# An RWKV-7 and convolution layer on one core: head pairs given in two parts, the LayerNorm 60 priorities later, the bonus product behind the keys

## The chip, the core and the metric

The kernel runs on one core of one Trainium2 chip. A time is the device time of one execution in microseconds (us). The kernel before took 2864.6 us, the median of three runs (2861.78 to 2865.63). The two kernels compute the same outputs from the same inputs.

## What is computed

One layer works on 2048 new tokens of 1024 channels, and on one token more for each of 8 older sequences. In the reference, cut to what matters here:

```python
h = rms_norm(x, norm_pre_g)
proj = h @ w_in                      # r, k, v, z, two lora inputs, conv input, gates
ps = ps + (ps_prev - ps) * mu_shift  # token shift on r, k, v, z and the lora inputs
w_raw = decay_w0 + tanh(wl) @ decay_w2;  decay = exp(-exp(-softplus(-w_raw) - 0.5))
iclr = sigmoid(iclr_a0 + al @ iclr_a2)
kk = k * k_k;  kk = kk * rsqrt(sum(kk * kk) + 1e-12)       # per head of 64 channels
k = k * (1 + (iclr - 1) * k_a)
# per head, token by token:
# S_t = S_(t-1) diag(w_t) + (S_(t-1) a_t) b_t^T + v_t k_t^T;  y_t = S_t r_t   (a = -kk, b = kk * iclr)
y_gn = group_norm(y_w)
bonus = sum(r * k * r_k) * v                               # per head
o_r = (y_gn + bonus) * silu(z)
c = causal_conv(u * sigmoid(u2), 31 taps);  c = swish(layer_norm(c)) * silu(z_c)
y = sigmoid(g_r) * (o_r @ w_branch_r) + sigmoid(g_c) * (c @ w_branch_c)
x = x + rms_norm(y @ w_out, norm_post_g)
```

## The kernel before

The 2048 tokens are taken in four blocks of 512, and the 16 heads in eight pairs of 128 channels, so there are 32 units of one head pair in one block. Below, "pair 17" is unit 17 of 32, counted from 0: block 2, pair 1. The large products (gemms) run in three passes on a high and a low part of each operand; the weights are split by ScalarE and VectorE in block 0 and read back split in the later blocks. A gemm matmul into a pg bank (`pg<-ht,w`) needs nothing that a pair computes, and so can fill TensorE's time between a pair's steps; "filler" means such matmuls.

`stage_first` normalises block 0: it squares eight tiles of x on ScalarE and sums them over the channels with matmuls by `avg_c` into the bank `py`. `unit_in` computes r, k, v and z of a pair (a gemm and the token shift for each). `unit` does the pair: two small gemms with `lora_w`; the decay as a scan on VectorE (L522); the sum for kk by a matmul with `ones_b` (pa<-tmp,ones_b, the kk statistic); the scaled keys `ar` and `bk`; the bonus statistic (pa<-raw,ones_b) and its product `bonv` with v; silu(z) on ScalarE into a `keep` tile; four transposes of V (pb<-ident,raw); the keys' products (pa<-ar,bk), which VectorE masks into `sc` (sc<-pa,maskw); products into `aw`; transposes of `bk` (pa<-ident,bk), which ScalarE copies into `sc` (sc<-pa); a triangular inverse, done by VectorE row by row (gd, zr, gp; the last transposes are L609 and L611) and by two small products (pb<-gd,sc and pb<-zbuf,gp, the first and second inverse product, with ScalarE's copies gp and zbuf). Its second part is pa<-aw,zbuf, whose results ScalarE copies to pz and xv; pa<-sc,pz; pc<-xv,sc; then the chain of eight chunk states (pc<-xs,aw on TensorE and L691 on VectorE in turn), the outputs into py, and the GroupNorm (py<-gt,cent and pc<-gt,ones_b).

Between the pairs stand the fillers of the lists FILL0 to FILL2: conv inputs ("u"), gates (digits), conv gates ("z", "Z") and the channel LayerNorm of the convolution ("n", `conv_norm`): a matmul with avg_c for the mean (pg<-tmp,avg_c), four subtractions on VectorE, four squares on ScalarE, three adds on VectorE, and a second matmul with avg_c. The 31 taps of the convolution (et<-u,cw,et) are VectorE instructions that `pull` hands out between other steps.

The order on each engine is made by a scheduler at build time, from priorities: what the program gives first goes first when it is ready, `later(n)` moves what it holds n places back, and `behind` lets an instruction be issued only after a given one. Tiles with a tag have a fixed number of buffers (tmp 4, raw 8, keep 4, ar 2, sc 4, xv 2, bk and gd 1); the banks of PSUM are three pg, two pa, one pb, one pc and one py. A new tile of a tag waits until the oldest one is no longer read.

Of the kernel before, what the change touches and what calls it, by code (L numbers as in the profile page):

```python
# [11 lines left out]
ALU = mybir.AluOpType  # L12
# [4 lines left out]
GE, HPO, HPA = 4, 0, 0  # L17
LI = 1000
HP = 550
HPW, HPS, HPG, HPU, HPZ = HP, HP, HP, HP, HP  # L20
# [5 lines left out]
def rwkv7_conformer_step(  # L26
# [362 lines left out]
    def stage_first():  # L389
# [21 lines left out]
        for kt in range(KT):  # L411
            for i, src in enumerate((h9, sh)):
                nc.tensor.transpose(out=psv[:, kt, i, :], in_=src[0:NS, kt * 128:kt * 128 + 128],
                                    identity=ident[0:NS, 0:NS])
        pm = pyt()
        for kt in range(KT):
            sq = new([128, BS], "tmp")
            act(sq, xts[kt], AF.Square)
            mm(pm, avg_c, sq, start=(kt == 0), stop=(kt == KT - 1))
        rb = new([128, BS], "tmp")  # L420
        rsqrt(rb, pm, eps_rms, scale=float(DC) / D)
        ht = [new([128, 2, WX], "ht", F32R) for _ in range(KT)]
# [57 lines left out]
    count = [0]  # L480
    chains = []

# [16 lines left out]

    def unit(b, j, tw, ins):  # L500
        u = count[0]
# [23 lines left out]
        act(em, sw, AF.Exp, scale=DECAY)  # L525
        c3 = lambda t: t.rearrange("p (c t) -> p c t", c=NC)
        act(ep[:, :, 1:C + 1], c3(sw), AF.Exp, scale=-DECAY)
# [16 lines left out]
        stt(R, R, pv("rk", j), K, ALU.mult, ALU.mult)  # L544
        bonv = new([128, BS], "keep")
        mul(bonv, stat(pa, ones_b, R), V)
        sz = new([128, BS], "keep")
# [5 lines left out]
        ps = pb()  # L553
        with behind(*chains[-2:-1]):
            for c2 in range(NC // 2):
                nc.tensor.transpose(out=ps[:, c2 * 128:c2 * 128 + 128], in_=V[:, c2 * 128:c2 * 128 + 128],
                                    identity=ident)
        xv = new([128, NC, 2, C], "xv")
# [84 lines left out]
        for hf in range(2):  # L643
# [6 lines left out]
            for e, es in enumerate(ES):  # L650
                cp(W[hf][es, :, 1, 0:64], psv[ES[1 - e], :, 1, :])

        pull(UT)

# [33 lines left out]
        for c in range(NC):  # L688
            for e, es in enumerate(ES):
                last = mma(pu[es, c * C:c * C + C], MY[es, c, 0, :], xs[es, c, :], False)  # L690
            nc.vector.tensor_scalar(out=state[:, j, :] if c == NC - 1 else xs[:, c + 1, :], in0=pu[:, c * C:c * C + C],  # L691
                                    scalar1=dk[:, c:c + 1], scalar2=None, op0=ALU.mult)
        chains.append(last.ins)
        yps = pyt()
# [431 lines left out]
    def fill(b, ht, cs, what):  # L1126

        if what == "u":
            cs.append(glu(b, ht, len(cs)))
        elif what == "n":  # L1130
            while taps:
                pull(1)
            conv_norm(b, cs)
        elif what in "zZ":
            conv_gate(b, ht, cs, 2 * (what == "Z"))
        else:
            gate(b, ht, 2 * int(what))
# [22 lines left out]
    for b in range(NB):  # L1160
        last = b == NB - 1
        orr = []
        if b == SB - 1:
            work = sample_work()
            act(gate_s, gate_s, AF.Exp, scale=-1.0)
            act(gate_s, gate_s, AF.Ln, bias=1.0)
            act(gate_s, gate_s, AF.Exp, scale=-1.0)
        for j in range(HP):
            if j == RJ and not last:
                stage_rms(b + 1)  # L1170
            orr.append(unit(b, j, tw, ins))
            pull(FT)
            if j < HP - 1:
                ins = unit_in(b, j + 1, ht)
            for what in (FILL0 if b == 0 else FILL2 if last else FILL1)[j]:
                fill(b, ht, cs, what)
                pull(FT)
            if b in DW:
                for _ in range(DW[b][j]):
                    with later(LD):  # L1180
                        next(work, None)
# [81 lines left out]
```

## Time and profile before

| | kernel before |
|---|---|
| median of 3 runs | 2864.6 us (2861.78 to 2865.63) |
| profiled execution, its own time | 2862.01 us |
| its span in the profile | 2860.2 us |
| TensorE matmuls busy (PE) | 2726.3 us, 95% |
| TensorE weight loads busy (PEld) | 2172.7 us, 76% |
| VectorE busy (DVE) | 1967.7 us, 69% |
| ScalarE busy (ACT) | 1319.3 us, 46% |
| mean granted TensorE clock | 0.983 of full speed |

The span is what the profiler shows between the first and the last instruction. The four blocks end at about 745, 1440, 2140 and 2860 us. In a row of the timeline the first number is the start in us from the start of the span, the second the length in us of the merged instructions, then engine, line, operation, the tiles (out<-in) with shapes, the count, and in brackets the idle time of the engine before it and what ended it.

### The profile page before, as it was taken

The numbers are of one execution on the slowest core, as the hardware profiler recorded it, in microseconds if no ns is written. First come the engines' busy times: TensorE is split into PE (matmuls) and PEld (weight loads), VectorE is DVE, ScalarE is ACT, GpSimd is POOL, SyncE is SP. The second block draws the span as 40 slices with busy tenths as digits, with TensorE's granted clock in tenths as the row PEclk, the third lists the DMA queues.
The fourth block names the chain that finished last, engine by engine and source line by source line (L and its number), as shares of the span: only waits on it lengthen the run. The fifth ranks groups of instructions, "written<-read, shape, count | busy, mean of one in ns | idle before, by whom it ended". The sixth has DMA issues, their size and how long they took to land.

```text
span 2860.2 us, 55924 instructions
## 1 busy us (share of the span) xinstructions
PE 2726.3 (95%) x22814; PEld 2172.7 (76%) x22814; DVE 1967.7 (69%) x4553; ACT 1319.3 (46%) x2783; POOL 16.1 (1%) x61
## 2 busy tenths in 40 slices
PE   7999889999999999997999989999999998999998
PEld 6888878877877767775787767777797775777777
DVE  5899896777877567677676677665865856666622
ACT  5555556553244465445213446546512355554521
POOL 0000000000000000000000000000000000000000
PEclk9999999999999999998999999999999998999999
DMA  6555653546874333444565435343465531333474
GB/s 207 198 170 179 207 183 124 185 159 217 304 255 145 101 135 115 136 158 135 168 231 209 136 103 164 107 136 130 161 225 195 202 100 62 107 119 108 154 238 162
DMA packets 157715, 466.91 MB, mean 163 GB/s; under 512 B 19793, under 2 KB 25154, under 8 KB 157451
## 3 DMA queue, kind: packets, MB, share of 16 engines
q1 hardware_dynamic: 154909, 454.23, 47.9%
q10 hardware_dynamic: 2550, 9.12, 0.8%
q8 instruction: 179, 2.93, 0.4%
q14 instruction: 77, 0.63, 0.1%
HBM read 350.41 MB, written 113.35 MB: 162 GB/s over the span
## 4 chain that ended last, share of the span: by engine, by line
PE 60%; DVE 24%; ACT 11%; DMA 3%; issue 2%; SPq 0%; POOL 0%; DVEq 0%; ACTq 0%; POOLq 0%
PE pg L112 36%; PE pa L112 11%; PE pc L112 4%; PE py L112 4%; DVE gd L100 4%; DVE zr L605 4%; DVE zr L106 3%; PE pb L112 2%; ACT tmp L94 2%; ACT sc L94 2%; DVE raw L106 2%; DVE et L106 1%; ACT zbuf L94 1%; ACT gd L94 1%; DVE gp L589 1%
## 5 line engine op out<-in xcount | busy, mean ns | idle before, releaser
L112 PE MATMUL pg<-ht,w 128*128 128x512 f32 (+1 forms) x7200 | 1516.2, 362 | 22.9 <-ACT ht L94 6.6
L112 PEld LDWEIGHTS pg<-ht,w 128*128 128x128 f32 x7200 | 1166.4, 189 | 262.0 <-issue 50.5
L106 DVE SCALAR_TENSOR_TENSOR et<-u,cw,et 128x512 f32<-128x512 f32 x480 | 358.6, 747 | 7.4
L94 ACT ACTIVATE raw<-pg,omm 128x512 f32<-128x512 f32 (+1 forms) x155 | 93.6, 604 | 269.5 <-PE pg L112 263.3
L94 ACT ACTIVATE tmp<-tmp 128x512 f32<-128x512 f32 (+1 forms) x305 | 185.8, 626 | 10.5 <-DVE tmp L522 5.0
L100 DVE TENSOR_TENSOR gd<-zr,gp 128x8 f32<-128x8 f32 (+14 forms) x480 | 179.5, 374 | 12.6
L112 PE MATMUL pg<-orr,w 128*128 128x512 f32 (+2 forms) x960 | 185.9, 350 | 0.0
L605 DVE TENSOR_REDUCE zr<-gd 128x2 f32<-128x8 f32 (+14 forms) x480 | 176.5, 368 | 12.4
L112 PEld LDWEIGHTS pg<-orr,w 128*128 128x128 f32 x960 | 154.8, 188 | 25.8 <-issue 0.5
L94 ACT ACTIVATE w<-wraw 128x512 fp32r<-128x512 f32 x162 | 100.8, 627 | 137.3 <-PE pg L112 92.2
L691 DVE TENSOR_SCALAR xs<-pc,dk 128x64 f32<-128x64 f32 x224 | 63.6, 284 | 122.2 <-PE pc L112 120.0
L100 DVE TENSOR_TENSOR w<-wraw,w 128x512 fp32r<-128x512 f32 x162 | 110.5, 686 | 48.1 <-ACT w L94 43.0
L112 PEld LDWEIGHTS pa<-ar,bk 64*64 64x64 f32 x2048 | 104.3, 137 | 51.0 <-issue 22.8
L106 DVE SCALAR_TENSOR_TENSOR raw<-pg,prm,raw 128x511 f32<-128x511 f32 (+1 forms) x185 | 103.4, 572 | 47.3 <-ACT raw L94 46.7
L112 PE MATMUL pa<-ar,bk 64*64 64x128 f32 x2048 | 128.1, 284 | 6.4 <-DVE keep L100 5.5
L100 DVE TENSOR_TENSOR aw<-pa,id 128x256 f32<-128x256 f32 x64 | 27.2, 424 | 146.3 <-PE pa L112 145.5
L106 DVE SCALAR_TENSOR_TENSOR zr<-zr,sub 128x5 f32<-128x5 f32 (+7 forms) x512 | 115.5, 226 | 13.7
L94 ACT ACTIVATE gd<-sc 32x128 f32<-32x128 f32 x256 | 78.5, 306 | 92.3 <-DVE sc L100 89.5
L94 ACT ACTIVATE x<-pg 128x512 f32<-128x512 f32 (+1 forms) x80 | 40.9, 511 | 169.6 <-PE pg L112 169.3
L100 DVE TENSOR_TENSOR sc<-pa,maskw 128x512 f32<-128x512 f32 x128 | 86.0, 687 | 34.4 <-PE pa L112 33.9
L100 DVE TENSOR_TENSOR x<-x,pg 128x512 f32<-128x512 f32 (+1 forms) x80 | 46.0, 577 | 76.8 <-PE pg L112 65.7
L94 ACT ACTIVATE sc<-pa 64x256 f32<-64x256 f32 (+1 forms) x192 | 72.9, 379 | 42.4 <-PE pb L112 39.4
(357 smaller groups left out, 3740.0 us busy)
## 6 DMA issues: line engine op xcount, KB each, us to landing
w<-kept_in SPq DMA_DIRECT2D x366, 512.0 KB
kept_in<-w SPq DMA_DIRECT2D x122, 512.0 KB
wraw<-in_w_in_dram SPq DMA_DIRECT2D x122, 256.0 KB
w<-kept_br SPq DMA_DIRECT2D x48, 512.0 KB
w<-kept_out SPq DMA_DIRECT2D x40, 512.0 KB
gate<-x SPq DMA_DIRECT2D x64, 256.0 KB
x<-gate SPq DMA_DIRECT2D x64, 256.0 KB
w<-kept_bc SPq DMA_DIRECT2D x24, 512.0 KB
```

Source lines behind the costliest of these rows:

```text
L94: return nc.scalar.activation(out=out, in_=in_, func=func, scale=scale, bias=bias, **kw)
L100: return nc.vector.tensor_tensor(out=out, in0=a, in1=b, op=op)
L106: return nc.vector.scalar_tensor_tensor(out=out, in0=a, scalar=s, in1=b, op0=op0, op1=op1)
L112: return nc.tensor.matmul(out=out, lhsT=lhsT, rhs=rhs, start=start, stop=stop, **kw)
L589: nc.vector.transpose(out=gp, in_=gd.rearrange("p c j -> p j c").unsqueeze(3).to_broadcast([128, 32, NC, 4]))
L605: nc.vector.tensor_reduce(out=zr[:, 0:n, t:t + 2], in_=pr[:, 0:n, :, 0:w], axis=AX.X, op=ALU.add)
L691: nc.vector.tensor_scalar(out=state[:, j, :] if c == NC - 1 else xs[:, c + 1, :], in0=pu[:, c * C:c * C + C], scalar1=dk[:, c:c + 1], scal ...
```

## The change

There are five edits. In `stage_first` the squares are added on VectorE and summed over the channels with one matmul, where eight accumulating matmuls were. `unit` is cut in two functions, `unit_a` up to the transposes of bk and `unit_b` from pa<-aw,zbuf on, and the program gives them in the order: second part of pair j, first part of pair j+1, inputs of pair j+2, fillers of j; before it was both parts of pair j, inputs of j+1, fillers of j. The V transposes no longer stand behind the chain of the pair before the last. The bonus statistic and its product move from ahead of silu(z) to the end of `unit_a`. The LayerNorm of the convolution is put under `later(60)`.

```diff
--- before.py
+++ after.py
@@ -16,6 +16,7 @@
 RJ = 3
 GE, HPO, HPA = 4, 0, 0
 LI = 1000
+LN = 60
 HP = 550
 HPW, HPS, HPG, HPU, HPZ = HP, HP, HP, HP, HP
 LN_EXP_SET = 6
@@ -412,13 +413,13 @@
             for i, src in enumerate((h9, sh)):
                 nc.tensor.transpose(out=psv[:, kt, i, :], in_=src[0:NS, kt * 128:kt * 128 + 128],
                                     identity=ident[0:NS, 0:NS])
-        pm = pyt()
+        rb = new([128, BS], "tmp")
         for kt in range(KT):
-            sq = new([128, BS], "tmp")
+            sq = rb if kt == 0 else new([128, BS], "tmp")
             act(sq, xts[kt], AF.Square)
-            mm(pm, avg_c, sq, start=(kt == 0), stop=(kt == KT - 1))
-        rb = new([128, BS], "tmp")
-        rsqrt(rb, pm, eps_rms, scale=float(DC) / D)
+            if kt:
+                tt(rb, rb, sq, ALU.add)
+        rsqrt(rb, stat(pyt, avg_c, rb), eps_rms, scale=float(DC) / D)
         ht = [new([128, 2, WX], "ht", F32R) for _ in range(KT)]
         for kt in range(KT):
             stt(xts[kt], xts[kt], pv("npre", kt), rb, ALU.mult, ALU.mult)
@@ -478,7 +479,9 @@
 
 
     count = [0]
-    chains = []
+
+    def c3(t):
+        return t.rearrange("p (c t) -> p c t", c=NC)
 
     def unit_in(b, j, ht, first=None):
         c0 = j * 128
@@ -497,7 +500,8 @@
         shift(b, vz, 24 + j, Zr)
         return R, K, V, Zr
 
-    def unit(b, j, tw, ins):
+    def unit_a(b, j, tw, ins):
+
         u = count[0]
         count[0] += 1
         c0 = j * 128
@@ -523,7 +527,6 @@
                                      initial=0.0, op0=ALU.mult, op1=ALU.add)
         em = new([128, BS], "tmp")
         act(em, sw, AF.Exp, scale=DECAY)
-        c3 = lambda t: t.rearrange("p (c t) -> p c t", c=NC)
         act(ep[:, :, 1:C + 1], c3(sw), AF.Exp, scale=-DECAY)
         dk = const.tile([128, NC], F32, name="dk", bufs=2)
         vcp(dk, ep[:, :, C])
@@ -542,8 +545,6 @@
         mul(bk[:, :, 1, :], c3(K), c3(em))
         mul(ar[:, :, 1, :], c3(R), ep[:, :, 1:C + 1])
         stt(R, R, pv("rk", j), K, ALU.mult, ALU.mult)
-        bonv = new([128, BS], "keep")
-        mul(bonv, stat(pa, ones_b, R), V)
         sz = new([128, BS], "keep")
         sigmoid(sz, Zr)
         mul(sz, sz, Zr)
@@ -551,10 +552,9 @@
         pull(UT)
 
         ps = pb()
-        with behind(*chains[-2:-1]):
-            for c2 in range(NC // 2):
-                nc.tensor.transpose(out=ps[:, c2 * 128:c2 * 128 + 128], in_=V[:, c2 * 128:c2 * 128 + 128],
-                                    identity=ident)
+        for c2 in range(NC // 2):
+            nc.tensor.transpose(out=ps[:, c2 * 128:c2 * 128 + 128], in_=V[:, c2 * 128:c2 * 128 + 128],
+                                identity=ident)
         xv = new([128, NC, 2, C], "xv")
         xvp = xv.rearrange("p (c i) e v -> p c i e v", i=2)
         psv = ps.rearrange("p (c e v) -> p c e v", e=2, v=C)
@@ -650,6 +650,13 @@
             for e, es in enumerate(ES):
                 cp(W[hf][es, :, 1, 0:64], psv[ES[1 - e], :, 1, :])
 
+        bonv = new([128, BS], "keep")
+        mul(bonv, stat(pa, ones_b, R), V)
+        return W, ar, aw, xv, zv, dk, bonv, sz
+
+    def unit_b(b, j, parts):
+
+        W, ar, aw, xv, zv, dk, bonv, sz = parts
         pull(UT)
 
         P = new([128, NC, C], "pz")
@@ -687,10 +694,9 @@
                 mma(pu[es, c * C:c * C + C], W[c // 4][:, c % 4, e, 0:64], xv[:, c, e, :], c == 0)
         for c in range(NC):
             for e, es in enumerate(ES):
-                last = mma(pu[es, c * C:c * C + C], MY[es, c, 0, :], xs[es, c, :], False)
+                mma(pu[es, c * C:c * C + C], MY[es, c, 0, :], xs[es, c, :], False)
             nc.vector.tensor_scalar(out=state[:, j, :] if c == NC - 1 else xs[:, c + 1, :], in0=pu[:, c * C:c * C + C],
                                     scalar1=dk[:, c:c + 1], scalar2=None, op0=ALU.mult)
-        chains.append(last.ins)
         yps = pyt()
         for c in range(NC):
             for e, es in enumerate(ES):
@@ -1130,7 +1136,8 @@
         elif what == "n":
             while taps:
                 pull(1)
-            conv_norm(b, cs)
+            with later(LN):
+                conv_norm(b, cs)
         elif what in "zZ":
             conv_gate(b, ht, cs, 2 * (what == "Z"))
         else:
@@ -1165,13 +1172,17 @@
             act(gate_s, gate_s, AF.Exp, scale=-1.0)
             act(gate_s, gate_s, AF.Ln, bias=1.0)
             act(gate_s, gate_s, AF.Exp, scale=-1.0)
+        parts = unit_a(b, 0, tw, ins)
+        ins = unit_in(b, 1, ht)
         for j in range(HP):
             if j == RJ and not last:
                 stage_rms(b + 1)
-            orr.append(unit(b, j, tw, ins))
+            orr.append(unit_b(b, j, parts))
             pull(FT)
             if j < HP - 1:
-                ins = unit_in(b, j + 1, ht)
+                parts = unit_a(b, j + 1, tw, ins)
+            if j < HP - 2:
+                ins = unit_in(b, j + 2, ht)
             for what in (FILL0 if b == 0 else FILL2 if last else FILL1)[j]:
                 fill(b, ht, cs, what)
                 pull(FT)
```

The order at three places follows. The first is TensorE at the end of block 1, from the GroupNorm of pair 14 (py<-gt,cent) to the keys of pair 15 (pa<-ar,bk); pa<-tmp,ones_b is the kk statistic, pa<-raw,ones_b the bonus statistic, pa<-ident,ar and pa<-xv,sc the products for aw. Before:

```order
L112 MATMUL py<-gt,cent 128x512
L112 MATMUL pc<-gt,ones_b 128x512
L112 MATMUL pa<-tmp,ones_b 128x512
L112 MATMUL pg<-ht,w 128x512 x3
L112 MATMUL pa<-raw,ones_b 128x512
L112 MATMUL pa<-ar,bk 64x128 x16
L112 MATMUL pg<-ht,w 128x512 x7
L112 MATMUL pa<-ar,bk 64x128 x16
L112 MATMUL pg<-ht,w 128x512 x3
L112 MATMUL pa<-ident,ar 64x64 x16
L112 MATMUL pa<-xv,sc 64x64 x16
```

After:

```order
L113 MATMUL py<-gt,cent 128x512
L113 MATMUL pg<-ht,w 128x512 x5
L113 MATMUL pc<-gt,ones_b 128x512
L113 MATMUL pg<-ht,w 128x512
L113 MATMUL pa<-tmp,ones_b 128x512
L113 MATMUL pg<-ht,w 128x512 x26
L113 MATMUL pa<-ar,bk 64x128 x2
L113 MATMUL pg<-ht,w 128x512 x6
L113 MATMUL pa<-ar,bk 64x128 x14
L113 MATMUL pg<-ht,w 128x512 x3
L113 MATMUL pa<-ar,bk 64x128 x16
L113 MATMUL pg<-ht,w 128x512 x3
```

Gemm matmuls stand where three or none stood ahead of the keys, and the bonus statistic no longer stands there.

The second is TensorE, and then ScalarE, around the second inverse product of pair 17 (pb<-zbuf,gp); pg<-ht,w are fillers, pb<-ident,raw V transposes of the next pair. TensorE before:

```order
L112 MATMUL pb<-gd,sc 32x32 x16
L112 MATMUL pg<-ht,w 128x512 x7
L112 MATMUL pb<-zbuf_147,gp 32x32 x16
L112 MATMUL pg<-ht,w 128x512 x3
L112 MATMUL pa<-aw,zbuf_147 64x128 x16
L112 MATMUL pc<-xv,sc 64x64
L112 MATMUL pa<-sc,pz 64x128 x16
L112 MATMUL pc<-xv,sc 64x64 x15
L112 MATMUL pc<-xs,aw 64x64 x2
```

TensorE after:

```order
L113 MATMUL pb<-gd,sc 32x32 x16
L113 MATMUL pg<-ht,w 128x512 x7
L113 MATMUL pb<-zbuf_147,gp 32x32 x16
L113 MATMUL pa<-raw,ones_b 128x512
L556 MATMUL pb<-ident,raw 128x128 x2
L113 MATMUL pa<-aw,zbuf_147 64x128 x16
L113 MATMUL pc<-xv,sc 64x64
L113 MATMUL pa<-sc,pz 64x128 x8
L113 MATMUL pc<-xv,sc 64x64 x4
L113 MATMUL pa<-sc,pz 64x128 x8
L113 MATMUL pc<-xv,sc 64x64 x11
L113 MATMUL pc<-xs,aw 64x64 x2
```

ScalarE before, from the copies of gp on; sc<-pa are copies of the bk transposes, raw<-pg a token shift's first half:

```order
L94 ACTIVATE gp<-pb 32x256 x2
L94 ACTIVATE sc<-pa 64x4x64 x2
L94 ACTIVATE sc<-pa 128x4x64
L94 ACTIVATE sc<-pa 64x4x64
L94 ACTIVATE zbuf_147<-pb 32x8x32 x2
L94 ACTIVATE sc<-pa 64x4x64
L94 ACTIVATE raw<-pg,omm 128x512
L94 ACTIVATE zr<-grp 128x8x4
L94 ACTIVATE pz<-pa 128x256
L94 ACTIVATE xv<-pa 64x4x64 x2
L94 ACTIVATE pz<-pa 128x256
L94 ACTIVATE xv<-pa 64x4x64 x2
```

ScalarE after; keep<-raw and keep<-keep are silu(z) of the next pair:

```order
L95 ACTIVATE gp<-pb 32x256 x2
L95 ACTIVATE sc<-pa 64x4x64 x2
L95 ACTIVATE sc<-pa 128x4x64
L95 ACTIVATE sc<-pa 64x4x64
L95 ACTIVATE zbuf_147<-pb 32x8x32 x2
L95 ACTIVATE sc<-pa 64x4x64
L95 ACTIVATE zr<-grp 128x8x4
L95 ACTIVATE raw<-pg,omm 128x512
L95 ACTIVATE keep<-raw 128x512
L95 ACTIVATE pz<-pa 128x256
L95 ACTIVATE xv<-pa 64x4x64 x2
L95 ACTIVATE keep<-keep 128x512
```

On TensorE the bonus statistic and two transposes stand where three fillers stood; on ScalarE silu(z) of the next pair has come between the copies of the bk transposes and the second pz.

The third is the LayerNorm on TensorE (pg<-tmp,avg_c, its two matmuls) in block 2, behind the bk transposes (pa<-ident,bk), before:

```order
L646 MATMUL pa<-ident,bk 128x128 x4
L112 MATMUL pg<-ht,w 128x512
L646 MATMUL pa<-ident,bk 128x128 x4
L112 MATMUL pg<-ht,w 128x512 x26
L112 MATMUL pg<-tmp,avg_c 128x512 x2
L112 MATMUL pg<-ht,w 128x512 x15
L112 MATMUL pb<-gd,sc 32x32 x16
L112 MATMUL pg<-ht,w 128x512 x8
```

After:

```order
L646 MATMUL pa<-ident,bk 128x128 x4
L113 MATMUL pg<-ht,w 128x512 x4
L646 MATMUL pa<-ident,bk 128x128 x4
L113 MATMUL pg<-ht,w 128x512
L113 MATMUL pg<-tmp,avg_c 128x512 x2
L113 MATMUL pg<-ht,w 128x512 x83
L113 MATMUL pb<-gd,sc 32x32 x16
L113 MATMUL pg<-ht,w 128x512 x6
```

The two matmuls stand together in both, with the gemm matmuls behind them in the second and mostly ahead of them in the first.

## Rows read from the trace of the kernel before

**Rows 1.** The page's first part: the span, and the busy time and share of each engine with its instructions.

```profile
span 2860.2 us, 55924 instructions
...
PE 2726.3 (95%) x22814; PEld 2172.7 (76%) x22814; DVE 1967.7 (69%) x4553; ACT 1319.3 (46%) x2783; POOL 16.1 (1%) x61
```

**Rows 2.** TensorE's waits, grouped by what waits for what: us in total, times, longest in us.

```profile
PE pg L112 <- DVE tmp L100: 24.3, 7, 9.2
PE pa L112 <- DVE raw L106: 15.5, 8, 6.9
PE pa L112 <- ACT zbuf L94: 12.9, 28, 1.3
PE pb L112 <- DVE gd L609: 12.8, 17, 2.0
PE py L112 <- ACT tmp L94: 7.5, 1, 7.5
...
PE pb L112 <- ACT gp L94: 2.0, 3, 1.5
PE pa L112 <- ACT xv L94: 1.8, 4, 1.0
```

**Rows 3.** Stretches of the span, block 1 and the inverse of pair 7: length, busy time (and instructions) of TensorE's matmuls, its weight loads, VectorE, ScalarE and GpSimd, granted clock, DMA share, GB/s.

```profile
745.00:1440.00 695.00, 667.59 (x5254) 511.25 (x5253) 481.68 (x1106) 315.55 (x665) 2.70 (x8) 0.98 0.48 161
```

```profile
610.00:640.00 30.00, 24.74 (x177) 20.95 (x172) 28.31 (x76) 9.82 (x19) 0.34 (x1) 0.89 0.44 138
```

**Rows 4.** The timeline of the start: the sum of squares on TensorE, squares on ScalarE (tmp<-x), the root (tmp<-py) and the first gemm.

```profile
15.75 0.63 ACT L94 ACTIVATE tmp<-x 128x512 f32<-128x512 f32 x1 [0.98 <-PE py L112]
17.44 8.30 PE L112 MATMUL py<-tmp,avg_c 128*128 128x512 f32 x12
19.56 0.63 ACT L94 ACTIVATE tmp<-x 128x512 f32<-128x512 f32 x1 [1.30 <-PE py L112]
21.26 0.63 ACT L94 ACTIVATE tmp<-x 128x512 f32<-128x512 f32 x1 [0.56 <-PE py L112]
25.79 0.69 ACT L94 ACTIVATE tmp<-py,eps_rms 128x512 f32<-128x512 f32 x1 [3.11 <-PE py L112]
28.75 0.63 PE L112 MATMUL pg<-ht,w 128*128 128x264 f32 x3 [3.00 <-ACT ht L94]
```

**Rows 5.** TensorE at the end of block 1: two waits on the timeline, then two stretches with the columns of rows 3.

```profile
1318.66 0.96 PE L112 MATMUL pg<-ht,w 128*128 128x512 f32 x3 [1.96 <-ACT ht L94]
1326.19 2.08 PE L112 MATMUL pa<-raw,ones_b 128*128 128x512 f32 x2 [6.56 <-DVE raw L106]
```

```profile
1296.00:1335.00 39.00, 27.33 (x283) 18.02 (x281) 23.73 (x45) 24.64 (x50) 0.00 (x0) 0.78 0.21 67
```

```profile
1320.00:1330.00 10.00, 3.81 (x24) 2.02 (x26) 10.00 (x17) 4.91 (x8) 0.00 (x0) 0.52 0.07 22
```

**Rows 6.** The LayerNorm's two matmuls in block 0 and its second in block 2, and the stretch after the first of them.

```profile
419.71 1.02 PE L112 MATMUL pg<-tmp,avg_c 128*128 128x512 f32 x2
...
429.92 2.08 PE L112 MATMUL pg<-tmp,avg_c 128*128 128x512 f32 x2 [9.19 <-DVE tmp L100]
```

```profile
1708.82 2.07 PE L112 MATMUL pg<-tmp,avg_c 128*128 128x512 f32 x2 [7.38 <-DVE tmp L100]
```

```profile
430.00:440.00 10.00, 9.73 (x103) 7.56 (x105) 2.52 (x6) 5.68 (x15) 0.34 (x1) 0.51 0.01 2
```

**Rows 7.** The timeline around the two inverse products of pair 17.

```profile
1650.88 0.69 PE L112 MATMUL pb<-gd,sc 32*32 32x32 f32 x32 [0.97 <-DVE gd L609]
...
1651.51 1.88 PE L112 MATMUL pg<-ht,w 128*128 128x512 f32 x7
...
1652.50 0.77 ACT L94 ACTIVATE gp<-pb 32x256 f32<-32x256 f32 x2
1653.29 1.55 ACT L94 ACTIVATE sc<-pa 64x256 f32<-64x256 f32 x4
...
1653.32 0.69 PE L112 MATMUL pb<-zbuf,gp 32*32 32x32 f32 x32
...
1654.87 0.77 ACT L94 ACTIVATE zbuf<-pb 32x256 f32<-32x256 f32 x2
...
1655.29 2.36 PE L112 MATMUL pa<-aw,zbuf 64*64 64x128 f32 x32 [0.39 <-ACT zbuf L94]
...
1656.79 0.75 DVE L106 SCALAR_TENSOR_TENSOR raw<-pg,prm,raw 128x511 f32<-128x511 f32 x1 [5.48 <-ACT raw L94]
1656.82 0.38 ACT L94 ACTIVATE pz<-pa 128x256 f32<-128x256 f32 x1
...
1657.45 0.21 DVE L106 SCALAR_TENSOR_TENSOR raw<-carry,prm,raw 128x1 f32<-128x1 f32 x1
...
1657.58 0.33 PE L112 MATMUL pc<-xv,sc 128*64 128x64 f32 x2
```

**Rows 8.** Groups of instructions by line and form: busy us, mean ns of one, idle before. ScalarE's copies, the bonus product of VectorE (an add of that size takes as long), and its conv taps.

```profile
L94 ACT ACTIVATE raw<-pg,omm 128x512 f32<-128x512 f32 x96 | 65.8, 685 | 244.5 <-PE pg L112 238.7 <-DVE raw L106 4.7 <-PE pa L112 0.5
...
L94 ACT ACTIVATE keep<-raw 128x512 f32<-128x512 f32 x32 | 19.7, 616 | 0.0
```

```profile
L100 DVE TENSOR_TENSOR keep<-pa,raw 128x512 f32<-128x512 f32 x32 | 21.9, 686 | 11.4 <-PE pa L112 11.2
```

```profile
L106 DVE SCALAR_TENSOR_TENSOR et<-u,cw,et 128x512 f32<-128x512 f32 x480 | 358.6, 747 | 7.4
```

## The prediction

> **What bounds the kernel now.** I began with the page's busy shares: TensorE 95% of the span, VectorE 69%, ScalarE 46% [rows 1]. So TensorE sets the pace, and a change that keeps its work the same can win only idle time of TensorE: 2860.2 - 2726.3 = 133.9 us. The list of its waits came next, because it says who ends them [rows 2]: sums for the channel LayerNorm 24.3 us, the bonus statistic 15.5, the copies after the second inverse product 12.9, the last step of VectorE's triangular inverse 12.8, the first sum of squares 7.5. The reader is to see that no wait is long for its kind except the first two and the last; the others are half a microsecond or one in each of 32 pairs. Third, the timeline at the places that the change touches [rows 4 to 7].
>
> A rule speaks against reading 95% as a wall. The Trainium skill, page "Perfetto Trace Analysis", section "Identifying the Most-Contended Engine", calls matmul busy time a poor measure of headroom and weight-load busy time a good one; the latter is 76% in [rows 1]. By matmul busy time the ceiling of the gain is 133.9 us, by weight loads some 687 us. The change takes no matmul out of the steady part, so the smaller ceiling is the one it can reach, and no term below hangs on this.
>
> **The change part by part.** The sum is made against the profiled execution, 2862.0 us (1.8 us around its span of 2860.2); the median of the runs shown, 2864.6, is 2.6 us above it, and is added at the end.
>
> *Start.* Eight squares went into eight accumulating matmuls. The last twelve of their sixteen records took 8.30 us, 0.69 each, and ended at 25.74; three squares on ScalarE waited 0.98, 1.30 and 0.56 us for them, since only four buffers exist [rows 4]. Now seven adds, 0.69 us each as a product of that shape [rows 8], on VectorE take the squares as they come, and one matmul (two records, 1.4 us) follows. The last square, which ended at 21.89, comes up to 2.84 us earlier, at 19.05; one add and the matmul end at 21.1 where 25.7 stood: -4.6. Bounds: -2.5 (squares no earlier, adds behind VectorE's weight splits of 0.69) and -7. I take **-5**, since the adds have gaps of VectorE around them.
>
> *End of block 1.* Before, TensorE had hardly a filler between this pair's chain and the next pair's keys: it waited 1.96 and 6.56 us, the latter for the bonus statistic's operand, which stands ahead of the keys in its order [rows 5]. From 1296 to 1335 us it was idle 39.0 - 27.3 = 11.7 us [rows 5], of the 27.4 of the whole block [rows 3]. After, the order has 26 + 6 gemm matmuls between the kk statistic and the second batch of keys, 7.5 us at 0.234 each ((1.88 - 0.25) / 7 in [rows 7], 0.25 being the drain), the bonus no longer stands there, and VectorE's row of operations on x and ht has moved into the inverse of that pair. The stretch of that pair's inverse then holds seventeen other full-width VectorE operations and 90 gemms. Pair 17, with one such operation and 70 gemms, idled 0.97 us [rows 7]: sixteen more are 11 us, twenty gemms more are 4.7, so up to 7 us of idle belong to the price; as some of them stand in gaps of VectorE, I take 5. With 1.5 us of smaller waits just before 1296 that also go, 11.7 + 1.5 - 5: **-8** (bounds -12 and -3). The granted clock in 1320 to 1330 was 0.52 [rows 5], the lower level of 1.2 GHz, after these waits; 3.8 us of matmuls ran at it. Without the wait half of that comes back: **-2** (0 to -4). Block 3 has the same place; there the order keeps only 2.8 + 0.9 us of gemms, and I book nothing.
>
> *Stretches of the inverse.* In pairs 1 to 4 ten more conv taps of 0.747 and three operations of 0.69 stand between masks and inverse, 9.5 us, and 74 more gemm matmuls of 0.124, 9.2 us: +0.5 each, +2. Pair 7, idle 5.3 us from 610 to 640 [rows 3], had seventeen full-width operations besides and now has six, and 40 more gemms: -4. Pair 25 has 15 matmuls fewer (-3.5 us of cover) with the same VectorE work, and pair 23 has 66 fewer and fourteen VectorE operations fewer, 15.4 against 9.8 us: about +3 and +2.5, as cover ran out by 1 to 2 us before. Sum **+3** (-4 to +10). What this rests on is the row of the wait for the last inverse step, 0.97 us in a normal pair [rows 7], 12.8 in all [rows 2].
>
> *LayerNorm.* Its two matmuls are given 60 priorities later. The wait comes from VectorE: the mean, four subtractions, three adds, then the second matmul, 9.19 and 7.38 us with VectorE's inverse between [rows 6]. In the new order the two still stand together with no gemm between them, in blocks 0 and 2 just after the key transposes, so the wait stays. **0** (-24 if it went, which is a rival below; +4 if the inverse's rows push the adds).
>
> *After the second inverse product.* This place occurs 32 times. Before, [rows 7]: pb<-zbuf,gp starts at 1653.32; ScalarE copies four key transposes of 0.38, then zbuf; pa<-aw,zbuf starts 0.04 us after the first zbuf copy, 1655.29, with 0.39 idle; pc<-xv,sc starts at 1657.58 with none. Now the bonus statistic stands first, and takes the pa bank that the first transposes have left; so pa<-aw,zbuf needs the other bank, and with it the last of ScalarE's copies. In 19 pairs five copies and two of zbuf are due after gp (7 x 0.385 = 2.70 us after 1653.27), in 13 pairs six (3.08): pa<-aw,zbuf starts 2.69 or 3.07 us after pb, 2.84 in the mean. The matmuls to fill it are 0.69 of pb and, by the new order, 1.36 us in the mean (bonus 0.86, a statistic of this size taking 1.02 with its drain [rows 6]; the rest V transposes or gemms). Idle 2.84 - 0.69 - 1.36 = 0.79, against 12.9 / 32 = 0.40 and a little for gp [rows 2]: +0.33 x 32 = +10.6. From below: if the bonus only fills the old wait, the 12.9 us go, -11. From above: no V transpose or gemm ready there, +25. I take **+7**, the middle of the two bounds, which also is near the row's own sum.
>
> *ScalarE ahead of pz.* Between its last copy and pz, ScalarE now does the next pair's silu(z) as well: in the typical pair a 0.69 raw<-pg, a 0.62 keep<-raw and 0.63 more [rows 8], where before there was 0.2 to 0.9. From last copy to pc<-xv,sc it needs those plus 0.38 (pz) and 0.48 (first xv with its release); TensorE has 2.36 us of pa<-aw,zbuf meanwhile [rows 7]. So what goes over 1.6 us is waited for: 0.3 in a pair with 1.9 us of them, nothing with 1.5. Over the new order's pairs this adds up to some 8 us, less the 1.8 of before [rows 2]: +6. From below 0 (pz is also bound by TensorE), from above +25 (rival A). I take **+3**. On ScalarE alone pz would be first by priority; its queue was filled before pz was ready.
>
> The rule on this is in the Trainium skill, page "TensorE: Matmul & The Clock Gate", section "Architectural detail: the array is 16× 32×32, not 1× 128×128": ScalarE and VectorE take their queue strictly in order. The trace agrees: pz starts at 1656.82 behind a raw copy though its operand was there by about 1656.5 [rows 7].
>
> *Boundaries between blocks.* The new block's first gemm follows the old block's last at once, where 3 to 13 us of other work stood: **+1** (0 to +5).
>
> Moved V transposes and bonus multiplication cost no TensorE or VectorE time of their own: they are the same instructions; the 0.69 us bonus product on VectorE has 1.1 us until the second half of pa<-aw,zbuf wants its bank. Where VectorE is late by more than that, this wait is late next.
>
> Sum: -5 - 8 - 2 + 3 + 0 + 7 + 3 + 1 = **-1**: 2861 for a profiled run, 2863.6 beside the median; I write **2863 us**. The time goes from few long waits into many short ones.
>
> **The rivals.** *A: ScalarE's queue governs the second part (slower).* A copy ahead of pz waits for VectorE, which has the bonus product 0.69, the shift 0.75 and its carry 0.21 in that place, 1.65 us in all [rows 7, 8]. If about half the pairs lose 1.2 us, this costs 16 x 1.2 = 19 more: 2882. It turns the result to slower once the place costs 0.23 us more per pair (7.3 us over 32). For it: ScalarE's row grew by two of 0.6 us just there. Against: keep<-raw reads a tile finished long before, in the order. *B: the second part costs nothing.* Bonus and transposes fill the 0.40 us that were idle, and pz comes when TensorE is ready anyway: without the 7 + 3, 2853. For it: 12.9 us of wait are there to be filled. Against: the bank. *C: LayerNorm's wait goes after all*, if VectorE reaches its sums before TensorE does: 24.3 us [rows 2] less, 2839. Against: the order. The granted clock after that wait, 0.51 [rows 6], says what more would come back, a few microseconds. *D: the fill does not reach the end of block 1* in time (the change does not do what it seems to): without the 11, 2873; I count it with A's share, being the smaller.
>
> **How the numbers follow.** A measurement here can tell about 0.2%, 5.7 us: under 2858.9 is faster, over 2870.3 slower. My forecast gets 0.45, spread by its unknown terms as 0.10 faster, 0.26 same, 0.09 slower; its own range is 2852 to 2875. A and D together 0.25 (0.23 slower, 0.02 same), B 0.23 (0.22 faster, 0.01 same), C 0.07 (faster). That gives 0.39 faster, 0.29 same, 0.32 slower. The range reaches from C's edge to A's: 2838 to 2882.
>
> **What would show it.** Right: the first pg<-ht,w starts near 24 us instead of 28.75; no wait above 5 us for the bonus operand in block 1; the wait of pa<-aw,zbuf, then ended by the copies of sc, sums to 20 to 28 us; pc<-xv,sc has a new wait of 0.2 to 0.4; LayerNorm's row stays at 20 to 28 us. Wrong: that row under 10 us (C), the pa wait under 13 (B), pc waits near 1 us or more in most pairs (A), TensorE's busy sum other than 2726 by over 10 us (the clock, then).

## The result and the profile after

The changed kernel took 2844.5 us, median of 6 runs (2840.43 to 2854.16), against 2864.9 for the kernel before in the same series (2861.78 to 2866.15): ratio 0.9933, with a 95% interval of 0.9915 to 0.9950. It is 20 us faster, where 2863, no change, was forecast; the wide range, 2838 to 2882, held it. The page of its profiled execution (2840.91 us):

```profile
span 2839.0 us, 55943 instructions
...
PE 2681.9 (94%) x22800; PEld 2127.1 (75%) x22800; DVE 1965.4 (69%) x4560; ACT 1320.4 (47%) x2783; POOL 16.1 (1%) x61
```

Beside [rows 1] the surprise is in one number: TensorE's busy time fell by 44.4 us, from 2726.3 to 2681.9, with only 14 records fewer, while its idle time rose by 23 us (2860.2 - 2726.3 = 133.9 before, 2839.0 - 2681.9 = 157.1 now). The change did not win idle time at all. TensorE's waits after it:

```profile
PE pb L113 <- DVE gd L609: 18.9, 18, 4.8
PE pg L113 <- DVE tmp L101: 18.2, 5, 7.4
PE pg L113 <- ACT ht L95: 14.7, 6, 3.3
PE pg L113 <- DVE x L101: 13.2, 2, 12.8
...
PE pa L113 <- ACT sc L95: 7.8, 18, 0.6
PE pa L113 <- DVE bk L101: 7.7, 5, 5.5
PE pb L556 <- ACT zbuf L95: 5.8, 15, 0.5
```

Against [rows 2], the bonus operand (15.5) and pa<-aw,zbuf waiting for zbuf (12.9) are gone; the LayerNorm (24.3) stands at 18.2; new are the copies of sc (7.8), the keys' operand bk (7.7) and the V transposes behind zbuf (5.8), and a wait near the end for x has grown from 2.3 to 12.8.

Which matmuls became shorter is seen in the groups by form: busy us, mean ns of one, idle before. The kernel before:

```profile
L112 PE MATMUL pa<-ar,bk 64*64 64x128 f32 x2048 | 128.1, 284 | 6.4 <-DVE keep L100 5.5 <-DVE sc L100 0.9
L112 PE MATMUL pa<-aw,zbuf 64*64 64x128 f32 x1024 | 79.6, 285 | 12.9 <-ACT zbuf L94 12.9
L112 PE MATMUL py<-tmp,avg_c 128*128 128x512 f32 x16 | 12.1, 921 | 7.5 <-ACT tmp L94 7.5
```

The changed kernel:

```profile
L113 PE MATMUL pa<-ar,bk 64*64 64x128 f32 x2048 | 104.1, 283 | 10.3 <-DVE bk L101 7.7 <-DVE sc L101 2.5
L113 PE MATMUL pa<-aw,zbuf 64*64 64x128 f32 x1024 | 63.1, 272 | 2.6 <-ACT sc L95 1.4
L113 PE MATMUL py<-tmp,avg_c 128*128 128x512 f32 x2 | 2.0, 1127 | 4.4 <-DVE tmp L101 4.4
```

The keys' products take 24 us less, pa<-aw,zbuf 16.5, the squares 10. (Counted without the overlap with the instructions ahead of them, the keys take 121.5 and 98.3 us, pa<-aw,zbuf 78.7 and 62.3; the expectations below use this count.) Of the keys, count and mean length of one instruction are the same; where these are equal and the busy time is less, more of them run at once. (For pa<-aw,zbuf, whose mean fell from 285 to 272 ns, the run with the pc bank will show another reason.)

The granted clock is not what shortened the keys. In the same count, but only over records that start at the full clock, one record of the keys costs 57 ns before and 47 after. The clock has a part in the time, though: in the six runs of the changed kernel its mean goes from 0.988 (2840.4 us) to 0.980 (2854.2). The two runs at 0.982 and 0.983 took 2846.7 and 2847.7 us, and the ten runs of the kernel before at these values, all from the series of the experiments, 2858.1 to 2863.6, so of the 20 us some 14 stand at an equal clock, an estimate from few runs.

The timeline of pair 17's keys, before:

```profile
1623.90 1.12 PE L112 MATMUL pa<-raw,ones_b 128*128 128x512 f32 x2 [0.26 <-DVE raw L106]
1624.95 1.95 PE L112 MATMUL pa<-ar,bk 64*64 64x128 f32 x32
1626.83 0.96 PE L112 MATMUL pg<-ht,w 128*128 128x512 f32 x3
1627.71 1.09 PE L112 MATMUL pa<-ar,bk 64*64 64x128 f32 x16
```

After:

```profile
1584.47 0.44 PE L113 MATMUL pa<-ar,bk 64*64 64x128 f32 x4
1584.84 1.19 PE L113 MATMUL pg<-ht,w 128*128 128x512 f32 x4
1585.95 1.09 PE L113 MATMUL pa<-ar,bk 64*64 64x128 f32 x28
1586.97 0.97 PE L113 MATMUL pg<-ht,w 128*128 128x512 f32 x3
1587.88 1.63 PE L113 MATMUL pa<-ar,bk 64*64 64x128 f32 x32
```

The first batch is 32 records (16 matmuls of two records each) in both. Before they took 1.95 us; after, 28 of them took 1.09. Each of these matmuls uses a quarter of the array, 64 rows by 64 columns. Naming the quarters a and b (rows of the pair's first head), c and d (of the second), the built programs give the keys of a pair in this order, a point standing for fillers, in 11 of the 32 pairs before (in 11 more, one head follows wholly behind the other) and in 28 after:

```
before  abababadcdcdcdbc.abababab.dcdcdcdc
after   ad.bcadbcadbcadbc.ababadcdcdbcadbc
```

In the records, one group starts every 0.109 us, whether it is of two quarters (a, b) or of four (a, d, b, c). The old order comes from a bank, as the built program of the run bonus_pg below shows. The two heads write two pa banks; before, the bonus statistic had taken one of the two just ahead of the keys, so the scheduler gave the first head's eight matmuls, a and b, while VectorE still read the bonus, and only then the second head's. With the bonus behind the keys both banks are free.

### The profile page after: what moved, and what is told of

The parts are those of the page before. It is cut to its first block, busy times and chain, and to the rows that moved or that the text cites. A ratio compares the mean times of both kernels' runs of the same rounds, so it can differ in the third digit from the quotient of the medians.

```text
span 2839.0 us, 55943 instructions
## 1 busy us (share of the span) xinstructions
PE 2681.9 (94%) x22800; PEld 2127.1 (75%) x22800; DVE 1965.4 (69%) x4560; ACT 1320.4 (47%) x2783; POOL 16.1 (1%) x61
## 4 chain that ended last, share of the span: by engine, by line
PE 52%; DVE 27%; ACT 13%; DMA 4%; issue 3%; SPq 0%; POOL 0%; DVEq 0%; ACTq 0%; POOLq 0%
PE pg L113 35%; PE pa L113 7%; DVE gd L101 5%; DVE zr L605 5%; PE pc L113 4%; PE py L113 4%; DVE zr L107 3%; DVE et L107 3%; ACT sc L95 2%; PE pb L113 2%; DVE raw L107 2%; ACT tmp L95 2%; ACT zbuf L95 2%; DVE w L101 1%; ACT xv L95 1%
## 5 line engine op out<-in xcount | busy, mean ns | idle before, releaser
L113 PE MATMUL pa<-ar,bk 64*64 64x128 f32 x2048 | 104.1, 283 | 10.3 <-DVE bk L101 7.7
L113 PEld LDWEIGHTS pa<-ar,bk 64*64 64x64 f32 x2048 | 80.0, 135 | 42.4 <-DVE bk L101 19.4
L113 PE MATMUL pg<-xv,w 128*128 128x512 f32 (+2 forms) x320 | 90.5, 356 | 13.2 <-DVE x L101 13.2
```

Source lines behind the costliest of these rows:

```text
L113: return nc.tensor.matmul(out=out, lhsT=lhsT, rhs=rhs, start=start, stop=stop, **kw)
```

## The experiments

Theory 1 (array quarters) is the one just told; theory 2 is the prediction's, that only idle time can move. All ratios below are to the kernel before on the same chip.

**The bonus moved alone.** In the kernel before:

```diff
-        bonv = new([128, BS], "keep")
-        mul(bonv, stat(pa, ones_b, R), V)
         sz = new([128, BS], "keep")
...
                 cp(W[hf][es, :, 1, 0:64], psv[ES[1 - e], :, 1, :])
+        bonv = new([128, BS], "keep")
+        mul(bonv, stat(pa, ones_b, R), V)
```

> The kernel before with one of the five edits: bonus statistic and product at the end of the pair's first part. Theory 1 (array quarters): the keys' products now come four quarters at a time, since both pa banks are free when they begin; their busy time falls from 121.5 to about 98 us and that of pa<-aw,zbuf from 79 to about 62, while idle time grows by 10 to 25; time 2842 to 2852. Theory 2 (idle time alone, as in the prediction): busy time stays at 2726 within 5, and the place after the second inverse product costs 7 to 11; time 2862 to 2876.

It took 2850.8 us beside 2866.0, ratio 0.9949 (0.9935 to 0.9963). Its groups of keys and pa<-aw,zbuf:

```profile
L112 PE MATMUL pa<-ar,bk 64*64 64x128 f32 x2048 | 105.0, 288 | 19.8 <-DVE bk L100 13.0 <-DVE sc L100 6.3
L112 PE MATMUL pa<-aw,zbuf 64*64 64x128 f32 x1024 | 64.5, 277 | 5.0 <-ACT sc L94 4.5
```

Busy time fell (100.1 and 63.7 in the expectation's count, 2698.9 in all), idle time rose by 19 us between matmuls: theory 1, and some three quarters of the whole gain by this edit alone.

**The keys given head by head.** The changed kernel, with the loops turned so that two quarters follow each other:

```diff
-            for i in range(4):
-                c = hf * 4 + i
-                for q in range(2):
-                    for e, es in enumerate(ES):
+            for e, es in enumerate(ES):
+                for i in range(4):
+                    c = hf * 4 + i
+                    for q in range(2):
```

> The changed kernel with the keys' products given head by head, so that matmuls of two quarters of the array follow each other instead of four; no instruction, wait or bank is added. Theory 1: the keys' busy time rises from 98 to 115 to 125 us; time 2857 to 2868. Theory 2: no change of busy time, 2841 to 2849.

2867.1 us, ratio 1.0003 (0.9991 to 1.0014), beside 0.9933 of the changed kernel: the whole gain is gone, with the bonus still behind the keys.

```profile
L113 PE MATMUL pa<-ar,bk 64*64 64x128 f32 x2048 | 127.6, 283 | 12.3 <-DVE bk L101 7.4 <-DVE sc L101 4.7
L113 PE MATMUL pa<-aw,zbuf 64*64 64x128 f32 x1024 | 65.4, 278 | 2.9 <-ACT sc L95 2.2
```

And in pair 17:

```profile
1607.54 0.44 PE L113 MATMUL pa<-ar,bk 64*64 64x128 f32 x4
1607.90 1.18 PE L113 MATMUL pg<-ht,w 128*128 128x512 f32 x4
1609.01 1.58 PE L113 MATMUL pa<-ar,bk 64*64 64x128 f32 x28
```

The same 28 records take 1.58 us instead of 1.09, and the group's busy time is back at 128 while that of pa<-aw,zbuf stays. No instruction or bank was added. At the full clock one record costs 57 ns again, as in the kernel before. This shows that the order by quarters is the cause. By the ratios it is worth 20 us here, and so it is at an equal clock: the seven runs at 0.982 and 0.983 took 2865.2 to 2869.7 us.

**The bonus put back alone.** The changed kernel with the two bonus lines back ahead of silu(z).

> The changed kernel with the bonus statistic and product back ahead of silu(z); the split of the pairs, the LayerNorm's priority, the freed V transposes and the start stay. Theory 1: keys back at about 121 us, pa<-aw,zbuf at about 79; time 2855 to 2866. Theory 2 (the split brings the gain): 2838 to 2850, busy time near that of the changed kernel.

2879.6 us, ratio 1.0041 (1.0028 to 1.0055): keys 129.1 and pa<-aw,zbuf 77.0 as theory 1 had it, but 14 us slower than the kernel before, outside both ranges. Its longest row of waits is `pa<-DVE raw` with 21.9 us, the bonus operand again. So the other four edits together are a loss as long as the bonus stands ahead of the keys; which of them loses was not tried. Some of the loss goes with the clock: the runs range from 2866.5 us at a mean granted clock of 0.984 to 2884.9 at 0.974.

**The bonus in another bank.** The kernel before, with one word changed:

```diff
-        mul(bonv, stat(pa, ones_b, R), V)
+        mul(bonv, stat(pgt, ones_b, R), V)
```

> The kernel before, with the bonus statistic where it was but in a pg bank instead of a pa bank. Theory 1: both pa banks are free for the keys, so their busy time falls by 15 to 23 us, pa<-aw,zbuf stays near 79; time 2840 to 2855, unless the fillers lose by the missing pg bank (then up to 2865 with the keys still shorter). Theory 2: only idle can move; keys stay at 121 us, time 2858 to 2870.

3376.3 us, ratio 1.1776 (1.1756 to 1.1796), far outside either. TensorE's waits say why:

```profile
PE pa L112 <- ACT tmp L94: 209.9, 25, 20.0
PE pa L112 <- DVE bk L100: 203.0, 63, 8.2
```

With a pg bank in the pair's own steps the scheduler made another order, in which TensorE stood without fillers for 413 us. The time tells nothing of the theories. The keys do: the built program gives their first batch by four quarters in all 32 pairs, by no other edit than the bank.

```profile
L112 PE MATMUL pa<-ar,bk 64*64 64x128 f32 x2048 | 147.0, 354 | 203.0 <-DVE bk L100 203.0
```

Their 142 us, in the expectation's count, come from the clock: 1034 of the 2048 records started at its lower level, behind these waits, and the mean length rose to 354 ns. The 1014 at the full clock cost 47 ns each, as in the changed kernel, so the part of theory 1 that concerns the keys holds here too.

**The program order.** The changed kernel with both parts of a pair given together as before, all else kept:

```diff
-            orr.append(unit_b(b, j, parts))
+            orr.append(unit_b(b, j, unit_a(b, j, tw, ins)))
             pull(FT)
             if j < HP - 1:
-                parts = unit_a(b, j + 1, tw, ins)
-            if j < HP - 2:
-                ins = unit_in(b, j + 2, ht)
+                ins = unit_in(b, j + 1, ht)
```

> The changed kernel with the program order of before (both parts of a pair, then the next pair's inputs, then fillers); start, LayerNorm's priority, freed V transposes and the bonus behind the keys stay. Theory S (the new order fills the end of block 1, as the prediction had it, 8 to 10 us): idle time of block 1 back up by 8 to 10, time 2851 to 2858. Theory N (with the bonus behind the keys that stretch is filled in either order): 2842 to 2848.

2856.2 us, ratio 0.9976 (0.9967 to 0.9984), some 12 us over the changed kernel: the time is theory S's. The place is not. From the end of the state chain of pair 7 to that of pair 15, which is block 1, TensorE idled 28.4 us here and 25.3 in the changed kernel, so 3 us came back and not 8 to 10; from the start to pair 7 it idled 66.4 us here and 49.6 there. Of single rows of waits the keys' operand grew most:

```profile
PE pa L113 <- DVE bk L101: 19.5, 12, 5.8
```

against 7.7 us in 5 waits in the changed kernel; of the three longest, 5.7, 5.8 and 4.6 us, one each stands in blocks 0, 1 and 3. By the ratios it is also some 8 us slower than the bonus moved alone, from which it differs by the start, the LayerNorm's priority and the freed V transposes. The next two runs point at the V transposes, which were not tried alone.

**The start alone.** The kernel before with the edit in `stage_first`.

> The kernel before with the start's edit alone. If TensorE's start sets the pace of what follows, the first gemm comes at 25.6 instead of 28.75 us as in the changed kernel, and the whole is 3 us shorter: 2860 to 2863 beside 2865. Rival: block 0 is held by something later (weights, VectorE), and the time stays within 1 us of the kernel before.

2864.2 beside 2863.7, ratio 1.0002 (0.9994 to 1.0011). The first gemm did come earlier. The changed kernel's timeline, which has the same start:

```profile
20.71 2.05 PE L113 MATMUL py<-tmp,avg_c 128*128 128x512 f32 x2 [4.38 <-DVE tmp L101]
...
25.64 1.03 PE L113 MATMUL pg<-ht,w 128*128 128x264 f32 x3 [2.88 <-ACT ht L95]
```

Beside 28.75 [rows 4] that is 3.1 us, but in the run alone pair 0 begins 3.4 us earlier than before, pair 5 1.5, pair 10 1.0, pair 12 0.2, and the last pair 3.0 later. From the start of pair 0 to the end, the kernel before and then the run alone, with the columns of [rows 3]:

```profile
63.97:2860.22 2796.25, 2677.54 (x22519) 2132.30 (x22517) 1935.83 (x4470) 1287.98 (x2717) 10.46 (x31) 0.98 0.49 163
60.60:2863.20 2802.60, 2684.15 (x22519) 2137.67 (x22517) 1934.86 (x4470) 1289.28 (x2717) 10.47 (x31) 0.98 0.49 162
```

TensorE's idle time is the same, 118.7 and 118.5 us, so no wait took the lead in this execution: the same 22519 records were busy for 6.6 us longer, at a mean granted clock of 0.980 over the span beside 0.983. Why the medians show no gain either stays open.

**The LayerNorm's priority.** The changed kernel with `LN = 0`.

> The changed kernel with LayerNorm's priority put back (0 instead of 60). By the prediction nothing changes (waits for the LayerNorm's sums 18 us as now): 2841 to 2848. Rival: the lower priority is worth some 5 us, as the waits fell from 24.3 to 18.2: 2848 to 2855.

2845.3 us, ratio 0.9933 (0.9921 to 0.9945), the same as the changed kernel. The edit has no effect on the time that these runs could tell.

**The end.** The changed kernel has a wait that no step of the prediction had, as the last block's gates are read back from DRAM:

```profile
2730.88 1.29 DVE L101 TENSOR_TENSOR x<-x,pg 128x512 f32<-128x512 f32 x2 [39.60 <-DMA x<-gate]
2731.62 0.80 PE L113 MATMUL pg<-xv,w 128*128 128x512 f32 x1 [12.75 <-DVE x L101]
```

Before, the same wait was 2.27 us:

```profile
2753.74 0.63 PE L112 MATMUL pg<-xv,w 128*128 128x512 f32 x1 [2.27 <-DVE x L100]
```

The longer wait came with the bonus moved alone too (11.6 us), and not with the start alone (2.3); it stayed with the bonus put back (11.6). SyncE's queue in the changed kernel, one row a group of issues, shows the load behind the last gates' writes and those of the final states:

```profile
2719.79 0.86 SPq L1011 DMA_DIRECT2D gate<-x  x2
2720.74 0.67 SPq L1153 DMA_DIRECT2D out_dram<-x  x1
2721.49 2.58 SPq L1159 DMA_DIRECT2D out_dram<-tmp  x1
2728.03 0.33 SPq L1027 DMA_DIRECT2D x<-gate  x1
```

First the states were given another buffer:

```diff
-        sf = new([64, HP, 2, 64], "x")
+        sf = new([64, HP, 2, 64], "sc")
```

> The changed kernel with the tile for the final states taken from the tag sc instead of x. If the last block's gates come back late because their x buffer waits for the slow write of the states, the 12.75 us wait of pg<-xv,w near the end falls to 2 to 5 us, and the time to 2833 to 2838. Rival: the gates' own write or the queue of weights holds the load: the wait stays over 9 us, 2842 to 2847.

2842.1 us, ratio 0.9922 (0.9911 to 0.9934); the wait fell to 10.2 us, as the rival had it. The buffer is a small part of it. Then, with that, the writes were taken out of SyncE's queue:

```diff
-            nc.sync.dma_start(out=gates[b][i0 + i], in_=s[:, i])
+            (nc.scalar if b == NB - 1 else nc.sync).dma_start(out=gates[b][i0 + i], in_=s[:, i])
```

> The changed kernel with the final states in an sc tile, and the last block's gate writes given by ScalarE's DMA queue instead of SyncE's. If those writes are late because they stand behind weight loads in SyncE's queue, the wait of pg<-xv,w near the end (12.75, 10.2 with the sc tile alone) falls under 4 us, and the time to 2833 to 2838. Rival: the loads back stand behind the same weights, wait over 8 us, 2840 to 2845.

2838.7 us, ratio 0.9910 (0.9893 to 0.9926), wait 8.9 us: between the two theories, nearer the rival's wait. The loads were still in SyncE's queue behind weight loads.

**The bank after the second inverse product.** The changed kernel with the bonus statistic in the pc bank (`stat(pct, ones_b, R)`).

> The changed kernel with the bonus statistic in the pc bank, so that pa<-aw,zbuf no longer needs the bank that ScalarE's last copies hold. If that wait is a real price (the prediction's +7), the wait for the sc copies (7.8 us) goes, pa<-aw,zbuf keeps its 62 us, and the time falls to 2835 to 2840. Rival: it only trades places, as pa<-aw,zbuf then starts with the first zbuf copy and waits inside for the second, busy 70 to 79 us as in the kernel before: 2841 to 2848.

2836.7 us, ratio 0.9902 (0.9887 to 0.9916): some 8 us less. The waits for the copies of sc fell from 7.8 to 2.8 us and those of the V transposes from 5.8 to nothing, but pa<-aw,zbuf waited for zbuf again and took its longer form:

```profile
L113 PE MATMUL pa<-aw,zbuf 64*64 64x128 f32 x1024 | 78.3, 283 | 13.7 <-ACT zbuf L95 10.7 <-ACT sc L95 2.8
L556 PE MATMUL pb<-ident,raw 128*128 128x128 f32 x128 | 24.8, 285 | 0.0
```

So the time was as the first theory had it and the busy time as the rival had it. A row of pa<-aw,zbuf that is 15 us longer did not make the kernel slower, and in pair 17 its records show why: as in the kernel before, two of one head come first and the rest 0.24 us later, when the other head's zbuf is there. The busy time that the row lost in the changed kernel was at least in part waiting. That the 8 us are the price of the bank is not shown: idle time between the second inverse product and the chain fell by 8.0 us over all pairs (22.6 to 14.6), but pa<-aw,zbuf took 15.4 more in the expectations' count, so the gain came out elsewhere.

**A version that beats both.** Bonus in the pc bank, states in an sc tile, the last block's gate writes and the loads of its first two merges on ScalarE's queue:

```diff
+        q = nc.scalar if b == NB - 1 and m < 2 else nc.sync
-        nc.sync.dma_start(out=s, in_=gates[b][m])
-        nc.sync.dma_start(out=c, in_=gates[b][KT + m])
+        q.dma_start(out=s, in_=gates[b][m])
+        q.dma_start(out=c, in_=gates[b][KT + m])
```

> The changed kernel with the bonus statistic in the pc bank, the final states in an sc tile, the last block's gate writes on ScalarE's queue and the first two merges' gate loads there too. If the bank (7.8 us by the run alone) and the end (up to 10 us) are separate places, their gains add: the wait of pg<-xv,w under 3 us, 2824 to 2832. Rival: the end is held by the DMA queues' load in either case and the wait stays over 8 us: 2832 to 2838.

2823.4 us (2821.72 to 2826.66), ratio 0.9864 (0.9847 to 0.9880): by the ratios 20 us under the changed kernel. The wait at the end is down to 1.3 us, and the two gains add: 11 us by the ratios under the run with the pc bank, where that wait was 11.7.

```profile
span 2821.4 us, 55922 instructions
...
PE 2678.4 (95%) x22800; PEld 2132.8 (76%) x22800; DVE 1952.4 (69%) x4560; ACT 1318.3 (47%) x2783; POOL 16.1 (1%) x61
```

## Why the prediction was right or wrong

**The step that failed** is the first one: that a change which keeps TensorE's work the same "can win only idle time of TensorE", and with it that the moved bonus costs and brings nothing but its own instructions. The instructions were the same; the time that they took was not. The head-by-head run puts 20 us on the order of the keys by quarters, as much as the whole gain. One of the prediction's own signs of being wrong came true, a busy sum other than 2726 by over 10 us (2681.9), but it laid that to the clock. That the range held the time was luck: its lower edge is rival C's, whose LayerNorm wait did not go. The sign was there to be read before: two heads, two banks, one of them taken by the bonus just ahead. The place where the order was shown ahead of the prediction (the end of block 1) has 16 + 16 keys before and 2 + 14 + 16 after, but not which quarter each uses.

**Array packing.** The Trainium skill, page "TensorE: Matmul & The Clock Gate", section "Part 3: Packing small matmuls — row/col tiling", says that matmuls at different tile positions run at once in the array. The trace agrees, with one group each 0.109 us, of two or of four matmuls; the 20 us are from the runs.

**End of block 1, -8 and -2**: right in place, wrong in size. From the end of pair 14's state chain to that of pair 15's, before and after, with the columns of [rows 3]:

```profile
1310.00:1384.10 74.10, 61.83 (x551) 43.91 (x545) 63.43 (x138) 33.61 (x68) 0.34 (x1) 0.91 0.37 114
1263.50:1337.50 74.00, 65.16 (x571) 46.85 (x566) 51.61 (x117) 36.17 (x70) 0.34 (x1) 0.98 0.49 158
```

TensorE idled 12.3 and 8.8 us, -3.5 where -8 was forecast (27.4 and 25.3 over the block). The bonus wait went, but the next block's first gemms, now within the inverse of pair 15, wait for ht: 3.1, 2.2 and 0.9 us. The granted clock rose from 0.91 to 0.98 here, which is the -2 in kind; its size was not measured. What the split is worth by the unsplit run, some 12 us, is not at this place alone.

**After the second inverse product, +7**: near in idle time, wrong in what the place cost. Between pb<-zbuf,gp and pa<-aw,zbuf TensorE idled 12.9 us before and 17.1 after, +4.2 over all pairs; the wait that was to sum to 20 to 28 us is 7.8 (for sc) and 5.8 (the V transposes for zbuf). In pair 17 the step looks as forecast, with the mechanism that the prediction named:

```profile
1613.57 0.69 PE L113 MATMUL pb<-zbuf,gp 32*32 32x32 f32 x32
1614.38 1.12 PE L113 MATMUL pa<-raw,ones_b 128*128 128x512 f32 x2
...
1615.97 0.44 PE L556 MATMUL pb<-ident,raw 128*128 128x128 f32 x2 [0.47 <-ACT zbuf L95]
...
1616.37 1.96 PE L113 MATMUL pa<-aw,zbuf 64*64 64x128 f32 x32
...
1617.57 0.37 ACT L95 ACTIVATE pz<-pa 128x256 f32<-128x256 f32 x1
...
1618.27 0.33 PE L113 MATMUL pc<-xv,sc 128*64 128x64 f32 x2
```

pa<-aw,zbuf starts 2.80 us after pb, where 2.69 was worked out, and the wait is put down to the V transposes. But it lasts 1.96 us, not the 2.36 of [rows 7], which the sum took for its work. Before, it began with one head's zbuf copy and stood within itself until the other's came; that wait was shown as busy. Net of these 0.4 us a pair the place became cheaper, not dearer: -16.4 us of pa<-aw,zbuf against +4.2 of idle time.

**ScalarE ahead of pz, +3**: the idle time from pa<-aw,zbuf to the chain rose from 1.2 to 5.5 us over all pairs, +4.3; rival A's 1.2 us per pair did not come.

**LayerNorm, 0**: right for the edit. That its row fell from 24.3 to 18.2 came from elsewhere, since putting the priority back changes nothing.

**The start, -5**: the first gemm came at 25.64, not near 24: the sum of squares ended at 22.76, where 21.1 was worked out, as the last add ended at 20.57 and not 19.7 and the one matmul took 2.05 us and not 1.4. By the run alone none of the 3.1 us reached the end, so the step that failed is that an earlier start is an earlier end. In the executions that were profiled, matmuls that ran 6.6 us longer at a lower mean clock took the lead, not waits; the cause in the medians stays open.

**Stretches of the inverse, +3**: the row for gd rose from 12.8 to 18.9, +6, with its longest wait, 4.8 us, in pair 25 where it was expected.

**Not in the sum**: the wait at the end, 12.75 - 2.27 = +10.5 us.

Of the rivals, C (2839) and B (2853) had the right side, and the measured time lies between them, but for wrong reasons: the LayerNorm's row, which C had gone, stands at 18.2 us, and it was not idle places that filled themselves, but matmuls that ran side by side.

## What to carry to other kernels

Before counting a move as free, ask which banks it frees or holds, and whether small matmuls next to it use different parts of the array: their order can be worth more than any wait, and it shows as busy time, not as idle time. When the order of a program changes, look at its end for new waits, such as for a write and a read back through one DMA queue. And a busy row that begins with half of its operands holds a wait within it: compare its length in the pairs where all operands were there.

## What was not expected of the hardware

Four 64x64 matmuls of 128 columns on four quarters of the array started within 0.02 us, and the next group came 0.109 us after the first; two on two quarters had the same 0.109 us. So half of the array's pace was lost with TensorE shown busy at the full clock, and the page's 95% said nothing of it. The weight-load row did move: 2172.7 us before, 2127.1 after, with the keys' loads at 104.3 and 80.0.
